# Rows in runs of 16 m tiles, 36 longer transfers, and an earlier start of the engines, in a matmul-and-subtract kernel

**Chip, cores, metric.** One core of a Trainium2 chip. The time is device microseconds of one execution; every kernel was run several times beside the kernel before on the same chip. "Span" is the length of one execution in the record; each run's time is 1.7 to 1.9 us above its own span (2.0 to 2.1 in e10_order8).

## The reference

```python
batch, m, k, n = 16, 512, 1024, 768
x = randn(batch, m, k); weight = randn(k, n); sub_value = randn(batch, m, n)   # all float32
out = np.matmul(x, weight) - sub_value
```

Flattened, x is 8192 x 1024: 64 m tiles of 128 rows. The kernel reads 61.9 MB and writes 25.2 MB whatever its order, so the bytes of its loads and stores cannot be reduced.

## The kernel before

SyncE issues every transfer, in the order of one list: x tiles, weight chunks (`w`), sub tiles (`s`) and stores (`o`). ScalarE casts an x tile to fp16; TensorE transposes it (VectorE does so for two tiles in six); TensorE multiplies it with the resident weights; VectorE subtracts out of PSUM into the sub tile's own buffer, from which it is stored.

```python
S = 8                      # rows of a run: partition p holds the rows of S m tiles, one after the other
TRANSFERS = [              # (kind, first tile, tiles)
    ('x', 0, 1), ('w', 0, 1), ('x', 1, 1), ('w', 1, 1), ('x', 2, 1), ('w', 2, 1),
    ('x', 3, 2), ('w', 3, 1), ('s', 0, 1), ('x', 5, 3), ('s', 1, 3), ('x', 8, 4),
    # ... 38 in all, at most 8 tiles each ...
    ('o', 61, 2), ('o', 63, 1),
]
# ...
x_s = x_flat.rearrange("(s p j) k -> s p j k", p=P, j=S)     # the same for sub_value and out
section.enter_context(tc.tile_critical(no_gpsimd_drain=True))  # SyncE opens the section
# ...
# the operands of the idle matmuls, which keep TensorE busy until data is there: cleared by VectorE
dve.add(lambda: nc.vector.memset(idle_w, 0.0), then=count("idle"))
dve.add(lambda: nc.vector.memset(idle_x, 0.0), then=count("idle"))
# ...
idle(13)                  # 13 matmuls on zeros, a fourteenth follows below
cast(0)
# ...
# each of PE, DVE, ACT visits the block "past" at the end of its program once before its work:
with nc.body("turn_head", valid_engines=engines):
    nc.br_cmp(turn, 0, on_true="past", on_false="work", comp_op="IS_EQ", engines=engines)
with nc.body("work", valid_engines=engines):
    for q in (act, dve):
        q.emit(q.ops)
    # ... TensorE's program, most of it a loop over six tiles ...
with nc.body("past", valid_engines=engines):
    nc.regs_alu(turn, turn, 1, op=mybir.AluOpType.add)
    nc.br_cmp(turn, 2, on_true="turn_head", on_false="rest", comp_op="IS_LT", engines=engines)
```

Of the kernel before, what the change touches and what calls it, by code (L numbers as in the profile page):

```python
# [10 lines left out]
F32 = mybir.dt.float32  # L11
F16 = mybir.dt.float16

S = 8
NX, NSO = 16, 32
N16, NXT, NPT, NPO = 4, 4, 2, 3
N16P, NXTP = 2, 1
# [5 lines left out]
PER = 6  # L23
HEAD = 3
ON_DVE = frozenset(range(10, 60, 6))
HEAD_SLOT = None
LOOP = (4, 6, 10)

TRANSFERS = [
    ('x', 0, 1), ('w', 0, 1), ('x', 1, 1), ('w', 1, 1), ('x', 2, 1), ('w', 2, 1),  # L30
    ('x', 3, 2), ('w', 3, 1), ('s', 0, 1), ('x', 5, 3), ('s', 1, 3), ('x', 8, 4),
    ('s', 4, 4), ('x', 12, 4), ('s', 8, 8), ('x', 16, 2), ('x', 18, 6), ('s', 16, 8),
    ('x', 24, 8), ('o', 0, 8), ('s', 24, 8), ('x', 32, 8), ('s', 32, 8), ('x', 40, 8),
    ('o', 8, 8), ('o', 16, 8), ('s', 40, 8), ('x', 48, 8), ('s', 48, 8), ('x', 56, 8),
    ('o', 24, 8), ('o', 32, 8), ('s', 56, 8), ('o', 40, 8), ('o', 48, 8), ('o', 56, 5),
    ('o', 61, 2), ('o', 63, 1),
]


class Queue:  # L40
# [28 lines left out]
    def emit_loop(self, bodies):  # L69
# [30 lines left out]

        with self.nc.Fori(0, len(bodies), engines=OrderedEngineSet([self.engine.engine]), head_slot=HEAD_SLOT):
            self.emit(first, value=lambda sem, v: regs[sem.name], after=after)
# [3 lines left out]
def kernel(  # L106
# [7 lines left out]
    nc = tc.nc  # L114
# [11 lines left out]

    x_s = x_flat.rearrange("(s p j) k -> s p j k", p=P, j=S)
    sub_s = sub_flat.rearrange("(s p j) n -> s p j n", p=P, j=S)
    out_s = out_flat.rearrange("(s p j) n -> s p j n", p=P, j=S)
    w_c = weight.rearrange("(c p r) n -> c p r n", p=P, r=2)  # L130

    section = ctx.enter_context(ExitStack())
    section.enter_context(tc.tile_critical(no_gpsimd_drain=True))  # L133

    def sbuf(name, shape, dtype):
        return ctx.enter_context(nc.sbuf_tensor(name, shape, dtype)).ap()
# [13 lines left out]
    idle_w = sbuf("idle_w", [P, P], F16)  # L150
    stub = sbuf("stub", [P, 2], F16)
    mark = sbuf("mark", [P, 1], F32)
    idle_x = sbuf("idle_x", [P, 512], F16)
# [8 lines left out]
    def count(name):  # L162
        so_far[name] += 1
        return (counter[name], 1)

    sp, pe = Queue(nc, nc.sync), Queue(nc, nc.tensor)
    act, dve, pool = Queue(nc, nc.scalar), Queue(nc, nc.vector), Queue(nc, nc.gpsimd)

    pool.add(lambda: nc.gpsimd.memset(ident, 0.0), then=count("ident"))  # L169
    pool.add(lambda: nc.gpsimd.affine_select(  # L170
        out=ident, in_=ident, compare_op=mybir.AluOpType.not_equal, fill=1.0, base=0,
# [52 lines left out]
    def issue():  # L224
        nonlocal known
        while todo:
# [30 lines left out]
            here = ring[:, at % size : at % size + n]  # L257
            there = view[at // S][:, at % S : at % S + n]
            waits = []
# [23 lines left out]
    def cast(mi):  # L283
# [4 lines left out]
        waits = [landed["x", mi]]  # L288
        if first in ON_DVE:
            if mi == first:  # L290
# [14 lines left out]
    def transposes(mi):  # L305
        def one(c):
            def f():
                waits = []
                if c == 0:
                    b, before = take("pt", NPT, mi)  # L310
                    waits.append((counter["cast"], cast_at[mi]))
                    if before is not None:
                        waits.append((counter["evac"], evac_at[before]))
                b = slot["pt", mi]
                words = pt_b[:, b].bitcast(F32)[:, c * P : (c + 1) * P]
                from_ = x16_b[:, slot["x16", mi]].bitcast(F32)[:, c * P : (c + 1) * P]
                last = c == n_c - 1
                pe.add(lambda: nc.tensor.transpose(words, from_, ident), waits, count("turn") if last else None)  # L318
                if last:
                    turn_at[mi] = so_far["turn"]  # L320
                    waits = [(counter["turn"], turn_at[mi])]
                    if mi - mi % 2 == EARLY:
                        if mi == EARLY:
                            take("xtp", NXTP, mi)
                        to = xtp_b[:, slot["xtp", EARLY], mi - EARLY]
                    else:
                        d, before = take("xt", NXT, mi)
                        if before is not None:
                            waits.append((counter["mul"], mul_at[before]))
                        to = xt_b[:, d]  # L330
                    act.add(lambda: nc.scalar.copy(out=to, in_=pt_b[:, b]), waits, count("evac"))  # L331
                    evac_at[mi] = so_far["evac"]
            return f
        return [one(c) for c in range(n_c)]

    def transposes_dve(mi):

        x16 = x16p_b[:, slot["x16p", mi]].bitcast(F32).rearrange("p j (c q) -> p (j c) q", c=n_c)
        blocks = [(a, b) for a in range(P // Q) for b in range(P // Q)]

        def one(n, a, b):
            def f():
                waits = []
                if n == 0:
                    d, before = take("xtp", NXTP, mi)
                    waits.append((counter["cast"], cast_at[mi + 1]))
                    if before is not None:
                        waits.append((counter["mul"], mul_at[before + 1]))
                xt = xtp_b[:, slot["xtp", mi]].bitcast(F32).rearrange("p j (c m) -> p (j c) m", c=n_c)
                last = n == len(blocks) - 1  # L350
                dve.add(lambda: nc.vector.transpose(  # L351
                    xt[b * Q : (b + 1) * Q, :, a * Q : (a + 1) * Q],
                    x16[a * Q : (a + 1) * Q, :, b * Q : (b + 1) * Q],
                ), waits, count("pair") if last else None)
                if last:
                    pair_at[mi] = so_far["pair"]
            return f
        return [one(n, a, b) for n, (a, b) in enumerate(blocks)]

    def matmuls(mi, c):  # L360
        first = mi - mi % 2
        on_dve = first in ON_DVE or first == EARLY
        waits = []
# [31 lines left out]
    def finish(mi):  # L395
        assert mi in done["s"]
        done["finish"].add(mi)
        o = so_ring[:, mi % NSO].rearrange("p (h n) -> p h n", h=2)
        po = po_b[:, slot["po", mi]]
        dve.add(lambda: nc.vector.tensor_tensor(  # L400
            out=o, in0=po[:, :, :NS], in1=o, op=mybir.AluOpType.subtract
        ), [landed["s", mi], (counter["mul"], mul_at[mi])], count("finish"))
        finish_at[mi] = so_far["finish"]
        issue()
# [1 line left out]
    issue()  # L406


    starts = len(dve.ops)
    dve.add(lambda: nc.vector.memset(idle_w, 0.0), then=count("idle"))  # L410
    dve.add(lambda: nc.vector.memset(idle_x, 0.0), then=count("idle"))  # L411
    dve.ops = dve.ops[starts:] + dve.ops[:starts]

    def idle(n):
        pe.add(lambda: nc.tensor.ldweights(idle_w, tile_position=(0, 0)), [(counter["idle"], 2)])  # L415
        for _ in range(n):
            pe.add(lambda: loaded_matmul(po_b[:, NPO - 1, 0], idle_w, idle_x, start=True, stop=True))

    def lead(mi):
        return LEAD_DVE if mi - mi % 2 in ON_DVE else TA + CA  # L420

# [51 lines left out]
    for mi in range(HEAD + (EARLY is not None), n_mt):  # L473
# [3 lines left out]
        t = mi + TA  # L477
        tr = transposes(t) if ahead <= t < n_mt and t - t % 2 not in ON_DVE else []
        for c in range(n_c):
# [9 lines left out]
        finish(mi)  # L489
        if mi + LEAD_TURN in ON_DVE:  # L490
            waiting += transposes_dve(mi + LEAD_TURN)
# [14 lines left out]
    with nc.body("turn_head", valid_engines=engines):  # L506
        nc.br_cmp(turn, 0, on_true="past", on_false="work", comp_op="IS_EQ", engines=engines)  # L507
    with nc.body("work", valid_engines=engines):
        for q in (act, dve):
            q.emit(q.ops)  # L510
        first, size, times = LOOP
        pe.emit(pe.ops[: marks[first]])
        ends = [marks[first + size * n] for n in range(times + 1)]
        pe.emit_loop([pe.ops[a:b] for a, b in zip(ends, ends[1:])])
        pe.emit(pe.ops[ends[-1] :])
        nc.br("past", engines=engines)
    with nc.body("past", valid_engines=engines):
        nc.regs_alu(turn, turn, 1, op=mybir.AluOpType.add)  # L518
        nc.br_cmp(turn, 2, on_true="turn_head", on_false="rest", comp_op="IS_LT", engines=engines)  # L519
    nc.switch_bb("rest")  # L520

    left = [one for one in lanes if not one["tags"] <= known]
    last = next(one for one in left if of_o[n_mt - 1] in one["tags"])
# [36 lines left out]
```

## Time and profile before

| | before |
|---|---|
| time, median of the six runs beside the kernel after | 210.94 us (210.65 to 211.54) |
| span of the profiled run | 208.7 us |
| TensorE busy, DMA queue busy | 94%, 97.9% |
| idle matmuls begin | 6.07 us |
| last matmul ends | 204.05 us |
| last subtraction ends, last store lands | 205.04 us, 207.4 us |

In the profiled run the last store, of one tile, needs 2.3 us from its issue to its landing, and from the landing to the end are 1.3 us. The profiled run took 210.46 us. The prediction shows the page's lines.

### The profile page before, as it was taken

The numbers are of one execution on the slowest core, as the hardware profiler recorded it, in microseconds if no ns is written. First come the engines' busy times: TensorE is split into PE (matmuls) and PEld (weight loads), VectorE is DVE, ScalarE is ACT, GpSimd is POOL, SyncE is SP. The second block draws the span as 40 slices with busy tenths as digits, with TensorE's granted clock in tenths as the row PEclk, the third lists the DMA queues.
The fourth block names the chain that finished last, engine by engine and source line by source line (L and its number), as shares of the span: only waits on it lengthen the run. The fifth ranks groups of instructions, "written<-read, shape, count | busy, mean of one in ns | idle before, by whom it ended". The sixth has DMA issues, their size and how long they took to land.

```text
span 208.7 us, 2630 instructions
## 1 busy us (share of the span) xinstructions
PE 196.2 (94%) x1234; PEld 75.6 (36%) x700; DVE 127.6 (61%) x218; ACT 108.9 (52%) x113; POOL 0.8 (0%) x7
## 2 busy tenths in 40 slices
PE   0899979999999999999999999999999999999991
PEld 0023324434433443443443344344344334434430
DVE  0231151995696599299469559929946955982331
ACT  2246478554762845557276284555727629434510
POOL 1000000000000000000000000000000000000000
PEclk9999999999999999999999999999999999999997
DMA  6999999999999999999999999999999999999985
GB/s 205 407 426 429 436 422 433 443 419 437 438 422 457 400 438 443 446 427 407 460 433 415 424 429 433 441 440 432 416 452 415 435 424 429 438 438 419 423 350 211
DMA packets 5476, 87.08 MB, mean 417 GB/s; under 512 B 608, under 2 KB 608, under 8 KB 1888
## 3 DMA queue, kind: packets, MB, share of 16 engines
q1 hardware_dynamic: 5472, 87.03, 97.9%
q14 instruction: 3, 0.02, 0.1%
q8 instruction: 1, 0.02, 0.0%
HBM read 61.87 MB, written 25.17 MB: 417 GB/s over the span
## 4 chain that ended last, share of the span: by engine, by line
PE 92%; ACT 3%; issue 2%; DVE 1%; DVEq 0%; SPq 0%
PE po_b L181 82%; PE pt_b L318 10%; ACT x_b L300 1%; ACT xt_b L331 1%; ACT xtp_b L331 0%; DVE so_ring L400 0%; DVE idle_x L411 0%; DVE idle_w L410 0%; DVEq L507 0%; DVEq L519 0%; DVEq L518 0%; DVEq L555 0%; DVEq L504 0%; SPq L133 0%
## 5 line engine op out<-in xcount | busy, mean ns | idle before, releaser
L181 PE MATMUL po_b<-w_sb,xt_b 128*128 128x384 f16 x704 | 125.9, 326 | 0.0
L400 DVE TENSOR_TENSOR so_ring<-po_b,so_ring 128x768 f32<-128x768 f32 x64 | 61.2, 958 | 60.0 <-PE po_b L181 53.8
L331 ACT COPY xt_b<-pt_b 128x1024 f16<-128x1024 f16 x44 | 44.5, 1012 | 80.3 <-PE pt_b L318 79.0
L351 DVE STREAM_TRANSPOSE xtp_b<-x16p_b 32x256 f32<-32x256 f32 x144 | 62.7, 435 | 2.2
L181 PE MATMUL po_b<-w_sb,xtp_b 128*128 128x384 f16 x320 | 61.3, 326 | 0.1
L380 PEld LDWEIGHTS <-xt_b 128*128 128x128 f16 x352 | 34.4, 98 | 57.2 <-issue 53.7
L318 PE MATMUL pt_b<-ident,x_b 128*128 128x128 f32 x184 | 47.6, 274 | 1.6 <-ACT x_b L300 1.4
L300 ACT CAST x_b<-x_ring 128x1024 f16<-128x1024 f32 x46 | 47.2, 1048 | 2.9 <-DMA x_ring<-in_x_dram 2.9
L318 PEld LDWEIGHTS pt_b<-ident,x_b 128*128 128x128 f32 x184 | 25.4, 141 | 46.1 <-issue 42.4
L380 PEld LDWEIGHTS <-xtp_b 128*128 128x128 f16 x160 | 15.7, 98 | 18.5 <-issue 16.4
L300 ACT CAST x16p_b<-x_ring 128x1024 f16<-128x1024 f32 x18 | 18.8, 1046 | 4.0 <-DMA x_ring<-in_x_dram 4.0
L181 PE MATMUL po_b<-idle_x,idle_w 128*128 128x512 f16 x26 | 9.2, 513 | 6.1 <-DVE idle_x L411 6.1
L248 DVE CAST w_sb<-so_ring 128x768 f16<-128x768 f32 x8 | 4.1, 556 | 9.6 <-DMA so_ring<-in_weight_dram 9.6
L410 DVE MEMSET idle_w<- 128x64 uint32 x1 | 0.1, 112 | 5.6 <-issue 5.6
L331 ACT COPY xtp_b<-pt_b 128x1024 f16<-128x1024 f16 x2 | 2.0, 1012 | 2.2 <-PE pt_b L318 2.2
L415 PEld LDWEIGHTS <-idle_w 128*128 128x128 f16 x4 | 0.4, 99 | 6.1 <-DVE idle_x L411 6.1
L300 ACT ACT_TABLE_LOAD x1 | 1.3, 1283 | 1.8 <-issue 1.8
L487 ACT CAST stub<-ident 128x1 f16<-128x1 f32 x2 | 0.4, 196 | 0.0
L170 POOL TENSOR_SCALAR_AFFINE_SELECT ident<-ident 128x128 f32<-128x128 f32 x1 | 0.3, 292 | 0.1
L411 DVE MEMSET idle_x<- 128x256 uint32 x1 | 0.3, 272 | 0.0
L464 POOL MEMSET mark<- 128x1 f32 x1 | 0.1, 99 | 28.6 <-ACT xtp_b L331 28.6
L169 POOL MEMSET ident<- 128x128 f32 x1 | 0.2, 204 | 0.5 <-SPq L133 0.5
(4 smaller groups left out, 0.4 us busy)
## 6 DMA issues: line engine op xcount, KB each, us to landing
so_ring<-in_sub_value_dram SPq DMA_DIRECT2D x7, 3072.0 KB, 24.3
out_dram<-so_ring SPq DMA_DIRECT2D x7, 3072.0 KB, 24.5
x_ring<-in_x_dram SPq DMA_DIRECT2D x5, 4096.0 KB, 20.7
x_ring<-in_x_dram SPq DMA_DIRECT2D x2, 2048.0 KB, 27.1
so_ring<-in_weight_dram SPq DMA_DIRECT2D x4, 768.0 KB, 9.6
x_ring<-in_x_dram SPq DMA_DIRECT2D x1, 3072.0 KB, 24.8
x_ring<-in_x_dram SPq DMA_DIRECT2D x2, 1024.0 KB, 23.2
out_dram<-so_ring SPq DMA_DIRECT2D x1, 1920.0 KB, 7.7
```

Source lines behind the costliest of these rows:

```text
L170: pool.add(lambda: nc.gpsimd.affine_select(out=ident, in_=ident, compare_op=mybir.AluOpType.not_equal, fill=1.0, base=0, pattern=[[-1, P]] ...
L181: return nc.tensor.add_instruction(mybir.InstMatmult(name=nc.get_next_instruction_name(), engine=full.engine, ins=list(full.ins), outs=lis ...
L248: lambda at=at, r=r, st=st: nc.vector.tensor_copy(out=w_sb[:, at, r], in_=st[:, r]),
L300: act.add(lambda: nc.scalar.copy(out=to, in_=x_in), waits, count("cast"))
L318: pe.add(lambda: nc.tensor.transpose(words, from_, ident), waits, count("turn") if last else None)
L331: act.add(lambda: nc.scalar.copy(out=to, in_=pt_b[:, b]), waits, count("evac"))
L351: dve.add(lambda: nc.vector.transpose(xt[b * Q : (b + 1) * Q, :, a * Q : (a + 1) * Q], x16[a * Q : (a + 1) * Q, :, b * Q : (b + 1) * Q],), ...
L380: pe.add(lambda weights=weights: nc.tensor.ldweights(weights, tile_position=(0, 0)), [w for w in waits if w[0] in ready])
L400: dve.add(lambda: nc.vector.tensor_tensor(out=o, in0=po[:, :, :NS], in1=o, op=mybir.AluOpType.subtract), [landed["s", mi], (counter["mul"] ...
L411: dve.add(lambda: nc.vector.memset(idle_x, 0.0), then=count("idle"))
L415: pe.add(lambda: nc.tensor.ldweights(idle_w, tile_position=(0, 0)), [(counter["idle"], 2)])
L487: lambda t=t: nc.scalar.copy(out=stub[:, t - n_mt : t - n_mt + 1], in_=ident[:, :1]), [(counter["ident"], 2)], count("cast")
```

## The change

Its intent: TensorE should start earlier (GpSimd clears the idle operands, VectorE's visit comes nearer, GpSimd lets the engines into the section), and the memory traffic should need fewer and longer transfers.

```diff
-S = 8
+S = 16
+NEAR = 140
 TRANSFERS = [
     ('x', 0, 1), ('w', 0, 1), ('x', 1, 1), ('w', 1, 1), ('x', 2, 1), ('w', 2, 1),
-    ('x', 3, 2), ('w', 3, 1), ('s', 0, 1), ('x', 5, 3), ('s', 1, 3), ('x', 8, 4),
-    ... 38 in all
+    ('w', 3, 1), ('x', 3, 2), ('s', 0, 4), ('x', 5, 2), ('x', 7, 5), ('s', 4, 4),
+    ('x', 12, 4), ('s', 8, 8), ('x', 16, 2), ('x', 18, 8), ('s', 16, 4), ('s', 20, 12),
+    ('x', 26, 6), ('o', 0, 16), ('x', 32, 5), ('s', 32, 6), ('x', 37, 6), ('x', 43, 5),
+    ('s', 38, 10), ('o', 16, 10), ('x', 48, 8), ('s', 48, 10), ('x', 56, 8), ('o', 26, 6),
+    ('o', 32, 16), ('s', 58, 6), ('o', 48, 10), ('o', 58, 4), ('o', 62, 1), ('o', 63, 1),
 ]
-    section.enter_context(tc.tile_critical(no_gpsimd_drain=True))
+    section.enter_context(tc.tile_critical(sync_engine=mybir.EngineType.Pool, no_gpsimd_drain=True))
+    pool.add(lambda: nc.gpsimd.memset(idle_w, 0.0), then=count("idle"))
+    pool.add(lambda: nc.gpsimd.memset(idle_x, 0.0), then=count("idle"))
-    dve.add(lambda: nc.vector.memset(idle_w, 0.0), then=count("idle"))     # (cut: moved to VectorE's front)
-    dve.add(lambda: nc.vector.memset(idle_x, 0.0), then=count("idle"))
-        for q in (act, dve):
-            q.emit(q.ops)
+        act.emit(act.ops)
+        dve.emit(dve.ops[:NEAR])
     nc.switch_bb("rest")
+    dve.emit(dve.ops[NEAR:])
```

## The prediction

> **What bounds the kernel now.** I read the busy shares first, then the stages, then the head of the chain of work that ended last, then single instructions of the head.
>
> The page's busy shares, its slices for the DMA, and its queue table:
>
> ```profile
> PE 196.2 (94%) x1234; PEld 75.6 (36%) x700; DVE 127.6 (61%) x218; ACT 108.9 (52%) x113; POOL 0.8 (0%) x7
> ...
> DMA  6999999999999999999999999999999999999985
> ...
> q1 hardware_dynamic: 5472, 87.03, 97.9%
> ```
>
> Two resources are full at once. TensorE is busy 94% of the span, and the DMA queue 97.9% of it. The stage table tells whether the DMA share is an average or holds everywhere (columns: stage, length, busy time of PE, PEld, DVE, ACT, POOL, granted clock, DMA share, GB/s):
>
> ```profile
> 0.00:20.00 20.00, 13.78 (x60) 2.98 (x28) 4.50 (x10) 7.65 (x8) 0.70 (x6) 1.00 0.92 365
> 20.00:40.00 20.00, 18.36 (x119) 7.39 (x70) 8.05 (x12) 13.40 (x15) 0.10 (x1) 1.00 1.02 431
> 40.00:80.00 40.00, 40.00 (x260) 15.93 (x147) 30.35 (x55) 22.82 (x24) 0.00 (x0) 1.00 1.01 431
> ...
> 120.00:160.00 40.00, 40.00 (x261) 16.23 (x150) 28.18 (x49) 24.17 (x25) 0.00 (x0) 1.00 1.01 433
> 160.00:200.00 40.00, 40.00 (x261) 16.12 (x149) 26.15 (x44) 19.88 (x23) 0.00 (x0) 1.00 1.00 429
> 200.00:209.00 9.00, 4.04 (x25) 1.08 (x11) 1.92 (x2) 0.00 (x0) 0.00 (x0) 0.86 0.58 239
> ```
>
> From 40 to 200 us TensorE is never idle, and from 20 to 200 us the DMA never is: it moves 429 to 433 GB/s in every stage, 431 on average. So neither bound has room in the middle. What can move lies in the first 30 us and in the last 6. The head of the chain:
>
> ```profile
> 1.04 0.06 DVEq L507
> 1.11 3.99 issue
> 5.10 0.05 DVEq L518
> ...
> 5.63 0.11 DVE idle_w L410
> 5.74 0.28 DVE idle_x L411
> 6.03 0.05 issue
> 6.07 6.09 PE po_b L181 x14
> 12.17 0.45 PE pt_b L318 x4
> ```
>
> VectorE jumps to the block at the end of its program (L507) and comes out of the jump 3.99 us later (L518). Only then does it clear the operands of the idle matmuls, so TensorE's fourteen idle matmuls begin at 6.07 us and hold it until 12.17, although the first x tile was cast by 6.95 us (cast from 5.91, 1.04 long). The first real transposes are therefore some 4 to 5 us late.
>
> **What the Trainium skill says.** "Runtime: NRT & Kernel Launch", section Instruction fetch mechanics: a taken branch to a target outside the resident window of two 16 KiB pages has to fetch the target before it goes on. The trace agrees with a stall of this kind: VectorE's jump costs 3.99 us, while ScalarE, whose program is shorter, is at the same block (1.0 to 1.4 us) within 0.4 us. "TensorE: Matmul & The Clock Gate", Part 1: a cold array runs at half rate and warms after about 3.4 us of activity counted in a free-running window. The trace agrees with the half rate, 6.09 us / 14 = 435 ns for an idle matmul of 512 columns at first and 1.24 us / 5 = 248 ns in the next group; it shows about 6 us to the change here. "DMA: Bandwidth & Descriptors", section Where 436 GB/s comes from: the SBUF side has a ceiling of 435 GB/s. The trace's 431 stands at 99% of that.
>
> **The change part by part.**
>
> *GpSimd clears the idle operands.* Two clears of 0.11 and 0.27 us leave VectorE, and GpSimd gets them ahead of its identity. GpSimd begins that identity at 0.94 us and clears 128x128 f32 in 0.20 us, so I estimate both clears done by 1.5 us. TensorE is through its own two branches at about 2.25 us (the second starts at 1.9, the longer takes 0.34). So the idle matmuls start at about 2.3 in place of 6.07: 3.75 us earlier. They end at about 8.4, after the cast at 6.95 and after w chunk 0 is cast at 8.82 or nearly.
>
> *VectorE visits mid-program.* Its first 140 operations come before the visited block and the rest after it, so the target is about as near as ScalarE's, whose visit is cheap. I expect the 4 us to vanish. Even if they stayed, nothing needs VectorE before w chunk 0 lands at 7.79.
>
> *GpSimd enters the section for all engines.* The five engines start at 0.8 to 0.9 us now; the gate moves from SyncE to GpSimd. I expect 0 to 0.1 us at the start, and at most 0.2 at the end, partly beside the last store.
>
> *The transfers.* The bytes are the same, 87.03 MB; there are 36 transfers in place of 38 (estimate, from the sizes of both lists). A line fits the arrivals in before: arrival = 5.5 us + MB queued up to and including it / 0.431. It gives 23.4 for x tiles 5 to 7 (7.73 MB; measured 6.70 + 16.7 = 23.4), 34.7 for sub tiles 4 to 7 (12.58 MB; measured 8.22 + 26.5 = 34.7) and 98.0 for x tiles 32 to 39 (39.85 MB; measured 73.42 + 24.6 = 98.0). For the new order:
> - w chunk 1 at 11.2, x tile 2 at about 12.4 and w chunk 2 at 14.3 are unmoved. With TensorE 3.75 us earlier, matmuls of chunk 1 (16.01 before) would start at 12.26; that chunk is cast by 12.23. Those of chunk 2 (19.04 before) would start at 15.29; it is cast at 15.38. So up to here 3.65 of the 3.75 us are kept.
> - w chunk 3 moves ahead of x tiles 3 and 4, which now land where the chunk did, at 18.7. Cast of tile 3 ends at 19.75, so its transposes start at 19.8 against 22.29: 2.5 us are kept.
> - Then the chain of before repeats: transposes, copy 1.01, cast 0.95, transposes of tile 4 at 22.4, copy to 24.1. x tiles 5 and 6 come at 5.5 + 8.39/0.431 = 25.0 (24.1 would have been wanted), cast to 25.95, transposes of tile 5 at 26.0 against 27.65: 1.65 us are kept.
>
> From there TensorE works without a gap, as now, so its last matmul ends at 204.05 - 1.65 = 202.4. I checked the later arrivals against this earlier clock with the same line. x tiles 32 to 36 come at 5.5 + 41.42/0.431 = 101.6, where ScalarE wants to cast tile 34 at 96.1. It stands for 5.5 us, but the copy behind it (tile 30) ends near 103.5, and matmuls of tile 30 start at about 105. So nothing reaches TensorE, with 1.5 us to spare.
>
> *The sum.* TensorE's side: 208.7 - 1.65 = 207.05 us of span. The DMA's side: at 200 us before had moved 7.31 + 8.62 + 17.24 + 17.29 + 17.33 + 17.15 = 84.94 MB (the stage rates, taken to two digits). The 2.09 MB left need 4.85 us at 431 GB/s, to 204.85. The last store takes 2.3 us from issue to landing, of which 0.9 is moving 0.39 MB, so 1.4 us follow: 206.25. From the last landing (205.1 + 2.3 = 207.4) to the end before has 1.3 us: 207.55. The later of the two sides rules, 207.55 at most; fewer short runs at the head (one sub transfer of four tiles for one of a single tile) may give some 0.2 back, so I take 207.2 to 207.5. The timed median lies 211.03 - 208.7 = 2.33 us above the span, which makes 209.5 to 209.8. I say 209.5.
>
> **The rivals.**
>
> *The whole head gain survives.* The 3.75 us at the start reach the end: about 207.3. For it speaks only that the idle matmuls are the first wait of the chain. Against it speak the arrivals above, and that the DMA would need 87.03 MB in 2 us less, at 435 GB/s or more, when no stage of before passes 433.
>
> *Nothing survives.* The DMA is the only bound, or TensorE's gain goes into waits for x: 211. For it: 97.9% of the queue busy. Against it: the last stage shows 239 GB/s, so the stores at the end wait for TensorE, and the DMA has about 2 us of slack there.
>
> *Runs of 16 rows change the rate of the memory.* Each partition's rows lie twice as far apart when a transfer has fewer than 16 m tiles. 1% of rate is 2 us, either way: 207.5 or 211.6. No view of before can tell.
>
> *The VectorE stall moves to mid-program.* If crossing into the last part costs the 4 us later, its transposes (they end at 46.6, wanted at 48.57: 2 us of slack) would make TensorE stand 2 us once: about 211.
>
> **Range and chances.** The main estimate 209.5 holds if the rate of before holds. Half a per cent of rate is 1 us; the head may be off by 1 us, as arrivals there are known to about 0.3 us and follow in a chain of casts. I put 8 in 10 on 207.5 to 211.2. Two per cent faster is below 206.81, which needs both the whole head gain and a rate above the ceiling of before: 0.05. Two per cent slower is above 215.25, which needs a stall that nothing shows: 0.02. Within: 0.93.
>
> **What would show it right or wrong.** Right: the idle matmuls begin near 2.3 us; no issue gap of 4 us at VectorE's visit; TensorE waits at tiles 3 and 5 for casts that wait for x; tile 5's transposes begin near 26.0; TensorE's last matmul ends near 202.4; the stages between 20 and 200 us stay at 429 to 435 GB/s; the final stage has a higher rate than 239. Wrong: a middle stage off 431 by over 1% (then the row runs matter), waits of TensorE after 40 us (a late x or sub transfer, or the stall moved), idle matmuls still near 6 us (TensorE's own branches or GpSimd are late), or an end that comes more than 1.5 us after the last landing (the GpSimd exit costs).

## The result and the profile after

| | before | after | predicted for after |
|---|---|---|---|
| time, median of six | 210.94 us | 211.12 us (210.83 to 211.30) | 209.5 us |
| idle matmuls begin | 6.07 | 2.06 | 2.3 |
| w chunk 0 has landed | 7.8 | 8.9 | 7.8 |
| last matmul ends | 204.05 | 203.27 | 202.4 |
| last subtraction ends | 205.04 | 204.26 | 203.4 |
| last store lands | 207.4 | 208.1 | 206.25 |
| span | 208.7 | 209.5 | 207.2 to 207.5 |

The ratio of after to before is 1.0005 (95% interval 0.999 to 1.002): the same. Ratios here are the mean time of one kernel's fast runs over that of the other's fast runs of the same rounds, so they are not quite the ratio of the medians quoted. The time forecast, 1.5 us less, was wrong, although 211.12 still lies inside the range.

TensorE did start 4 us earlier. The timeline of the head, kernel after (start, duration, engine, line, operation, and in brackets the idle time before it and what ended it):

```profile
0.97 0.20 POOL L169 MEMSET idle_w<- 128x128 f16 x1 [0.53 <-POOLq L133]
1.11 0.53 POOL L170 MEMSET idle_x<- 128x512 f16 x1
...
2.06 5.73 PE L183 MATMUL po_b<-idle_x,idle_w 128*128 128x512 f16 x14 [2.06 <-POOL idle_x L170]
...
8.94 1.03 DVE L250 CAST w_sb<-so_ring 128x768 f16<-128x768 f32 x2 [8.94 <-DMA so_ring<-in_weight_dram]
...
25.77 1.04 ACT L302 CAST x_b<-x_ring 128x1024 f16<-128x1024 f32 x1 [0.66 <-DMA x_ring<-in_x_dram]
```

The clears are done and the idle matmuls run by 2.06 us. VectorE is out of its jump at 1.6 us (5.1 before). But the first weight chunk is there at 8.94 us; the same line of before reads 7.79. The cast of x tile 5, which had been expected to start at 25.0 us, starts at 25.77.

The waits of TensorE, kernel after (engine, line, waited for, us in total, times, longest):

```profile
PE pt_b L320 <- ACT x_b L302: 3.1, 3, 1.7
PE po_b L183 <- POOL idle_x L170: 2.1, 1, 2.1
PE po_b L183 <- DVE w_sb L250: 1.1, 2, 0.7
PE po_b L183 <- DVE so_ring L402: 0.3, 1, 0.3
```

The one wait of 6.1 us for the idle operands has become 2.1 us. Other waits have taken back 3.1 of these 4 us: those for casts of late x tiles are 3.1 us (1.4 before), for weights 1.1 (none before), for a subtraction 0.3 (none before). From 40 us on there is no wait, as before. So TensorE keeps 204.05 - 203.27 = 0.78 us of its 4.

The stage table, kernel after, in the form that the prediction explains:

```profile
0.00:20.00 20.00, 16.14 (x74) 3.47 (x34) 4.11 (x8) 7.85 (x8) 1.30 (x8) 1.00 0.92 356
20.00:40.00 20.00, 17.06 (x109) 7.06 (x68) 7.92 (x12) 14.27 (x15) 0.10 (x1) 1.00 1.02 433
40.00:80.00 40.00, 40.00 (x259) 15.86 (x147) 31.10 (x56) 22.25 (x24) 0.00 (x0) 1.00 1.02 435
...
160.00:200.00 40.00, 40.00 (x260) 15.96 (x148) 25.21 (x42) 19.86 (x22) 0.00 (x0) 1.00 1.00 430
200.00:210.00 10.00, 3.26 (x21) 0.88 (x9) 1.92 (x2) 0.00 (x0) 0.00 (x0) 0.93 0.56 233
```

The rate from 20 to 200 us is that of before. The first stage moves 356 GB/s against 365, which is 0.18 MB or 0.4 us of transfer less. And the last stage, with 2.33 MB left (2.15 before), has no higher rate than before (233 over 10 us, 239 over 9).

Now the end. The last store, from the view of the DMA, before and then after (size, us from issue to landing):

```profile
out_dram<-so_ring SPq DMA_DIRECT2D x1, 384.0 KB, 2.3
```

```profile
out_dram<-so_ring SPq DMA_DIRECT2D x1, 384.0 KB, 3.9
```

After the change the last tile's store is handed over 0.8 us earlier and lands 0.8 us later: it stands 1.6 us behind other stores. The page's averages do not tell how this queue looks from inside. The trace does: it records sixteen increments of a semaphore for each transfer, one for each of the sixteen DMA engines. The table gives these sixteen landings for some transfers (worked out from the trace; MB is what the list has moved up to and including the transfer, two numbers where before and after differ):

| transfer | MB | before: first, middle, last | after: first, middle, last |
|---|---|---|---|
| w chunk 0 | 1.31 | 5.89, 6.25, 7.77 | 6.07, 6.37, 8.91 |
| x tiles 16, 17 | 18.87 | 47.31, 47.64, 49.43 | 47.69, 47.98, 50.26 |
| x tiles 56 to 63 | 68.16 / 69.73 | 161.43, 161.79, 163.53 | 165.44, 165.80, 168.09 |
| last store | 87.03 | 207.19, 207.28, 207.37 | 206.41, 206.51, 208.14 |

For most of the run fourteen of the sixteen landings are within 1 us of each other, while the last comes some 2 us (before) or 2.6 us (after) behind the first: at w chunk 0 it is 1.88 us in before and 2.84 in after. Towards the end a third one falls behind too. These increments do not name their engine; the packet records do, as shown under e8 below. A transfer counts as landed when the last engine has brought its share. In before the last store has its sixteen landings within 0.2 us, since the queue was empty when it came. In after, earlier stores are still under way on the late engine; the first engine is done at 206.4, the last one 1.7 us later. This is where the gain went.

### The profile page after: what moved, and what is told of

It is laid out like the page before. It is cut to its first block, busy times and chain, and to the rows that moved or that the text cites. A ratio compares the mean times of both kernels' runs of the same rounds, so it can differ in the third digit from the quotient of the medians.

```text
span 209.5 us, 2628 instructions
## 1 busy us (share of the span) xinstructions
PE 196.5 (94%) x1234; PEld 75.4 (36%) x700; DVE 126.9 (61%) x216; ACT 109.1 (52%) x113; POOL 1.4 (1%) x9
## 3 DMA queue, kind: packets, MB, share of 16 engines
q1 hardware_dynamic: 5184, 87.03, 97.7%
## 4 chain that ended last, share of the span: by engine, by line
PE 84%; DMA 9%; SPq 3%; ACT 1%; DVE 0%; issue 0%; POOLq 0%
PE po_b L183 75%; DMA x_ring<-in_x_dram 9%; PE pt_b L320 9%; SPq L283 2%; SPq L247 1%; ACT x_b L302 1%; DVE so_ring L402 0%; SPq L553 0%; POOLq L133 0%; POOLq L542 0%
## 5 line engine op out<-in xcount | busy, mean ns | idle before, releaser
L170 POOL MEMSET idle_x<- 128x512 f16 x1 | 0.5, 528 | 0.0
```

Of the source, the lines that this page charges most:

```text
L170: pool.add(lambda: nc.gpsimd.memset(idle_x, 0.0), then=count("idle"))
```

## The experiments

The theory that the experiments test (A): the end is set by the slowest DMA engine's stream of equal shares, and instruction fetches amid the first loads decide how late that engine starts. Rivals: the new rows and transfers eat the gain (B); the exit through GpSimd, or something after the stores, costs it (C).

All runs in one table. "w0" is the landing of w chunk 0; "sub" the end of the last subtraction, "store" the landing of the last store, both in the profiled run.

| run | w0 | sub | store | store - sub | median us | ratio to before (95%) |
|---|---|---|---|---|---|---|
| before | 7.77 | 205.04 | 207.37 | 2.33 | 210.94 | |
| after | 8.91 | 204.26 | 208.14 | 3.88 | 211.12 | 1.0005 (0.999 to 1.002) |
| e1_engines | 7.74 | 202.99 | 207.51 | 4.52 | 210.73 | 0.9993 (0.9982 to 1.0005) |
| e2_transfers | 8.82 | 204.68 | 208.19 | 3.51 | 211.20 | 1.0011 (0.9996 to 1.0025) |
| e3_visit_end | 8.76 | 204.10 | 208.09 | 3.99 | 211.20 | 1.0019 (1.0005 to 1.0034) |
| e4_clears | 8.45 | 203.75 | 207.67 | 3.92 | 210.78 | 0.9997 (0.9985 to 1.0009) |
| e7_rows | 8.68 | 204.83 | 208.46 | 3.63 | 211.60 | 1.0027 (1.0012 to 1.0043) |
| e10_order8 | 8.08 | 204.86 | 208.27 | 3.41 | 211.79 | 1.0039 (1.0006 to 1.0072) |
| e8_no_visit | 6.56 | 202.81 | 207.53 | 4.72 | 210.73 | 0.9987 (0.9954 to 1.002) |
| e12_after_no_visit | 6.81 | 204.42 | 208.53 | 4.11 | 211.42 | 1.0019 (1.0006 to 1.0031) |
| e11_late_start | 8.26 | 203.54 | 208.13 | 4.59 | 212.18 | 1.0064 (1.0048 to 1.0079) |
| e5_before_half | 7.71 | 203.70 | 206.03 | 2.33 | 209.22 | 0.9919 (0.990 to 0.9938) |
| e6_after_half | 8.99 | 204.34 | 206.67 | 2.33 | 209.73 | 0.9936 (0.9915 to 0.9957) |
| e9_engines_half | 7.63 | 202.82 | 205.16 | 2.34 | 209.18 | 0.9913 (0.9901 to 0.9926) |

The column "store - sub" is the test of what bounds the end. Where the queue is empty it is 2.33 us; everything above is waiting behind the late engine. "sub" moves over 2 us among the kernels with all their bytes, and "store" does not follow it. The last two stores show that the late engine has no gap there: in every kernel with all its bytes except before, the last landing of the last store comes 0.92 to 0.96 us after the last landing of the store ahead of it, and 0.39 MB at 431 GB/s take 0.9. In before it is 1.12 us: the late engine stood still for some 0.2 us (an estimate from these numbers), so in that run no more than this was to be won at the end without a shorter stream.

### The parts of the change, one at a time

**e1_engines**: the engine parts alone.

```diff
-S = 16            # and the 36 transfers
+S = 8             # and the 38 transfers of before; the rest as after
```

> The change's engine parts alone (GpSimd clears and gate, VectorE visits mid-program), with the rows and transfers of before. Theory A, the DMA stream sets the end: its slowest engine starts late because instruction fetches of the new visit come amid the first loads. Then w chunk 0 arrives near 8.9 us as after the change (7.8 before), TensorE's last matmul ends near 202 to 203, the last store lands near 208 and the time is 211.0 to 211.4, although the transfers are those of before. Theory B, the new rows and transfers eat the gain: then w chunk 0 arrives near 7.8, the span is about 207.2 and the time 209.3 to 209.8.

Measured: 210.73 us, ratio 0.9993. w chunk 0 came at 7.74 us (8.9 expected), so this part of theory A was wrong: the engine parts alone do not delay it. TensorE won 2.05 us, more than in the full change. Its last subtraction, and the last store's way:

```profile
202.03 0.96 DVE L403 TENSOR_TENSOR so_ring<-po_b,so_ring 128x768 f32<-128x768 f32 x1 [1.64 <-PE po_b L184]
```

```profile
out_dram<-so_ring SPq DMA_DIRECT2D x1, 384.0 KB, 4.5
```

All results are there at 202.99 us, 2.05 us before the kernel before has them, yet the last store lands at 207.51, 0.14 us later than before. Theory B predicted 209.8 or less for this run, and it has none of B's rows and transfers. B is out as the main cause: with the old transfers the gain is lost as well.

**e4_clears**: GpSimd's clears alone, all else as before.

```diff
-    dve.add(lambda: nc.vector.memset(idle_w, 0.0), ...)     # and idle_x
+    pool.add(lambda: nc.gpsimd.memset(idle_w, 0.0), ...)    # and idle_x; kernel before otherwise
```

> The kernel before with one part alone: GpSimd clears the idle operands; the visit at the end, the gate on SyncE, rows and transfers as before. Theory A: idle matmuls start near 2.1 us and TensorE ends 1.5 us or more before 204.05, yet the last store lands near 207.1 to 207.4 because the stream is full to its end; time 210.5 to 211.0, so under 0.3% faster. Theory B (the head gain is real and only the new transfers lost it): last store 2 us or more earlier, time 209.3 or less.

Measured: 210.78 us, ratio 0.9997; TensorE's end 1.3 us earlier (1.5 or more had been expected), the last store at 207.67, 0.3 us later than in before. The same picture: an earlier TensorE, and a store that does not come earlier.

**e2_transfers**: rows and transfers alone, engines of before. **e7_rows**: the rows alone.

```diff
-S = 8
+S = 16            # e2: also the 36 transfers; e7: the 38 transfers of before
```

> The change's rows and transfers alone, with the engines of before. Theory A: w chunk 0 arrives near 7.8 us as before, idle matmuls start near 6.1, the last store lands near 207.4 and the time is 210.7 to 211.1. Theory B: w chunk 0 arrives near 8.9 us and the time is 211.6 or more, as TensorE starts as late as before and the stream is slower too.

> The kernel before with runs of 16 rows alone, its own transfers kept. Theory A1, the row runs delay the first loads: w chunk 0 arrives near 8.8 us in place of 7.8, later arrivals are 0.5 to 1 us late, the last store lands near 208 and the time is 211.2 to 211.6. Theory A2, only the new order of transfers or chance of the instruction fetches delays them: w chunk 0 arrives between 7.7 and 8.5, the time is 210.7 to 211.0.

Measured: e2 at 211.20 us (1.0011), e7 at 211.60 us (1.0027). In both, w chunk 0 comes near 8.75 us, and the last store lands 0.8 and 1.1 us later than in before. The expectation of A for e2 missed; of B its late chunk came, and its time of 211.6 or more did not. A1 for e7 held. So the runs of 16 rows do cost something, at the head. The change is the sum of a part that wins nothing (engines, 0.9993) and rows that lose 0.3%; e2 against e7 suggests that the new list wins some 0.15% back, but the two ran on different chips and the intervals overlap, so that is not settled.

**e3_visit_end**: the kernel after, with VectorE's visit at the end of its program.

```diff
-NEAR = 140
+NEAR = 1000
```

> The kernel after, but VectorE visits the end of its program as before (all its operations before the visited block). Theory A: fetches fall as before, VectorE stands about 4 us in its jump but nothing needs it before 7.8 us; w chunk 0 arrives near 7.8, arrivals are about 0.5 to 0.9 us earlier than after the change, the last store lands near 207.2 to 207.5 and the time is 210.2 to 210.7. Theory B: w chunk 0 stays near 8.9 and the time at 211.1, within 0.2.

Measured: 211.20 us, w chunk 0 at 8.76. The expectation of A missed, and B's numbers came: the place of VectorE's visit makes no difference to the loads here. So for the end of the kernel theory A stands (e1, e4), while for the late head the 16-row runs are involved (e2, e3, e7 all have them, and w chunk 0 near 8.75). Whether through the fetches or by themselves is what e8 and e12 below tell apart.

### Is it the bytes?

**e5_before_half**, **e6_after_half**, **e9_engines_half**: three kernels (before, after, e1_engines) with half of the late sub columns not loaded. Their outputs are wrong, which doesn't matter for the times.

```diff
             there = view[at // S][:, at % S : at % S + n]
+            if kind == "s" and at >= 32:
+                here, there = here[:, :, : N // 2], there[:, :, : N // 2]
```

> The kernel before with the sub loads of tiles 32 to 63 cut to half their columns (6.3 MB or 14.6 us of transfer less; wrong result on purpose). Theory A, before is bound by TensorE and the DMA stream nearly together: TensorE's end stays at 204.0, the last store lands 2.0 to 2.3 us after the last subtraction, the span is 208.3 to 208.7 and the time 210.4 to 210.8: at most 0.2% faster. If the stream alone were the bound the time would fall by 2 us or more.

> The kernel after with the same cut (wrong result on purpose). Theory A, after is bound by the DMA stream at its end: TensorE's end stays near 203.3, but the last store now lands 2.0 to 2.3 us after the last subtraction in place of 3.9, so the span falls from 209.5 to 207.5 to 207.9 and the time to 209.6 to 210.1, 0.3 to 0.5% below the other half kernel. Theory C (the exit through GpSimd or something after the stores costs): time stays at 211.1.

> The change's engine parts with the transfers and rows of before, with the same cut (wrong result on purpose). Theory A: TensorE ends near 202.0, nothing holds the last store, the span is 206.3 to 206.7 and the time 208.4 to 208.9, about 1% below the kernel before: this is the head gain that the full stream of bytes hides. Theory C: 210.7 as without the cut.

Measured: 209.22, 209.73 and 209.18 us. In all three the wait behind other stores is gone (2.33 us, column "store - sub"). e6 came as expected, except that it was to be 0.3 to 0.5% faster than e5 and was 0.2% slower. It settles C: the exit is the same, and the time falls by 1.4 us. (With the gate on GpSimd the end comes 1.37 us after the last landing, with SyncE 1.30, in all runs to 0.01: the exit costs 0.07 us.)

The other two missed, each in a useful way. e5 fell by 1.9 us and not by 0.2, because TensorE's end came at 202.7 and not at 204.0. The head gives the likely reason. The first line is that of e5, the second that of the profiled run of before:

```profile
5.84 4.86 PE L181 MATMUL po_b<-idle_x,idle_w 128*128 128x512 f16 x14 [5.84 <-DVE idle_x L413]
```

```profile
6.07 6.09 PE L181 MATMUL po_b<-idle_x,idle_w 128*128 128x512 f16 x14 [6.07 <-DVE idle_x L411]
```

The same fourteen matmuls took 4.86 us here and 6.09 there (4.57 to 6.09 over all runs). They are slow until TensorE's clock rises (its warm-up), which came at 9.25 us in e5 and at 11.97 in before. TensorE's waits are otherwise nearly the same in both (5.8 and 1.4 us in e5, 6.1 and 1.4 in before). So the profiled run of before probably had a late warm-up, and in runs with an early one the DMA stream would hide TensorE's earlier end; that is inferred from this one pair of profiles. By the same pair, 1.3 of the 2.05 us that TensorE won in e1 against the profiled run of before may be no more than that. e9 was expected at 208.4 to 208.9 and came to 209.18, no faster than e5. Only its profiled run (208.34) showed the gain of the engine parts: 206.5 us of span against 207.3. So even without the DMA bound the head gain is 0.8 us in one pair of profiles and nothing in the medians; which of the two is typical stays open.

### Is it the instruction fetches?

**e8_no_visit**: e4_clears without any visit of a later block. **e12_after_no_visit**: the same edit in the kernel after.

```diff
-    nc.regs_mov(turn, 0)
+    nc.regs_mov(turn, 1)
```

> GpSimd's clears, rows and transfers of before, and no engine visits a later block at all. If instruction fetches amid the loads make one or two DMA engines lag, the fetches now come later and apart: the lag of the last of the sixteen engines at w chunk 0 falls below 1.3 us (1.5 in before, 1.9 with the clears alone) and rises by 0.4 to 1 us at each later fetch; the end depends on their number: 210.3 to 210.9. VectorE or ScalarE may stand some us at a fetch in mid-program, hidden or not. If fetches have nothing to do with the lag, it stays at 1.5 to 1.9 us at w chunk 0.

> The kernel after with no visit of a later block on any engine; rows and transfers as after. If its late first loads (w chunk 0 at 8.9 us) come from instruction fetches amid them, w chunk 0 arrives near 6.6 as without the visit on runs of 8 rows (6.56), and the lag of the last of the sixteen engines there falls from 2.5 us to 0.4; TensorE ends near 202; the fetches come later and the last store still lands at 207.4 to 208.1, time 210.6 to 211.1. If the runs of 16 rows themselves slow the first loads, w chunk 0 arrives at 7.3 or later with the sixteen engines close together.

The queues between 1 and 12 us, from the view of the DMA: kernel after first, then e8_no_visit (packets, MB, share of the sixteen engines):

```profile
q1 hardware_dynamic: 803, 3.67, 91.0%
q14 instruction: 2, 0.02, 0.6%
q8 instruction: 1, 0.02, 0.5%
```

```profile
q1 hardware_dynamic: 867, 4.01, 92.7%
```

Three instruction fetches (two of 8 KiB, one of 16 KiB) fall between the first loads of the kernel after; without the visit there is none, and 0.34 MB more data has been moved (0.17 MB more than in before, which has the list of e8). The head gains what the fetches had cost it, as both expectations said for that case: w chunk 0 is there at 6.56 us in e8 and 6.81 in e12, against 8.45 and 8.91 with the visits. Here the sixteen engines are within 0.64 and 0.79 us of each other.

The fetches are not gone, though; they come later. This is the same view of e8 between 29 and 35 us:

```profile
q1 hardware_dynamic: 203, 2.59, 102.1%
q8 instruction: 1, 0.02, 1.1%
```

One fetch of 16 KiB, at 30.9 us. The last of the sixteen landings was 0.42 us behind the middle in the transfer that landed at 29.6 us, and 1.41 us behind in the one at 34.3: a step of 1.0 us, and it stays.

The packet records tell which engine pays. In this stretch each packet starts within 0.02 us of the end of another one. Linked in this way they form sixteen chains, one for each DMA engine, and each chain carries eight packets of every transfer and one of 4 bytes. A fetch stands in one of the chains, in the place of data. In e8 the chain with the 16 KiB fetch goes from 0.07 us ahead of the middle one to 1.46 us behind it, a delay of 1.5 us; the 8 KiB fetches at 57.0, 79.5 and 160.9 us delay theirs by 0.9, 0.6 and 1.0. In the kernel after, the 16 KiB fetch of 5.18 us stands in the chain that is the latest from w chunk 0 to the end (2.2 to 2.4 us behind the middle), and the 8 KiB fetches of 4.64 and 162.8 us both stand in the second latest (1.1 us behind, then 2.1); the one of 3.32 us, amid the first transfer, leaves no lasting delay (0.1).

Fetches are not the whole lag. One chain without a fetch falls behind by up to 0.6 us with most of the stores: in e8 from the middle at 71 us to 1.9 us behind it at the end, in after to 1.8. In e8 two chains also lose 0.4 and 0.6 us between 176 and 183 us, where the trace shows no fetch. Why is not shown. By the end three chains of e8 are 1.9 to 2.2 us behind the middle (the last landing in before: 1.7), and the last store lands at 207.53.

So the fetches cause most of the last engine's lag (1.5 of its 2.2 us in e8), and where they come decides when it is paid. e8 has the earliest loads of all and an end at 210.73 us, the same as before. e12 is at 211.42: its last store, 208.53, is 0.4 us beyond what had been expected. TensorE ended at 203.42 and not near 202; its clock stood at 0.57 of full in the stretch from 25 to 29 us (as in e10 from 26 to 30), but the last store waits for the late engine all the same. That engine is 1.0 us behind that of e8 at the end. Half of it, 0.5 us, is there when x tile 1 lands (8.34 against 7.83), while the two lists are still the same. The gate differs as well, but over the other runs it is the rows that tell: the first of the sixteen landings of x tile 1 comes at 7.18 to 7.42 us with runs of 8 rows, whatever the gate (without e11, which starts late), and at 7.49 to 7.64 with runs of 16. So this is the cost of the 16-row runs on the first loads. Why rows twice as far apart slow them is not shown. The rest comes mostly with the fetches: the one of 16 KiB moves the last landing by 1.3 us here and by 1.0 in e8.

Rows and fetches together cost more than each alone. Without the visits w chunk 0 comes 0.25 us later with 16 rows (e12 against e8); with them it comes at 7.63 to 8.45 us in the kernels with 8 rows and at 8.68 to 8.99 in those with 16. Why they add up in this way is not shown either.

**e11_late_start**: e4_clears, with the first load held back until the clears are done, so that fetches come ahead of the data.

```diff
+            if (kind, at) == ("x", 0):
+                waits.append((counter["idle"], 2))
             sp.add(lambda here=here, there=there: nc.sync.dma_start(out=here, in_=there), waits, (sem, 16))
```

> The clears alone (e4_clears) with the first load held until GpSimd's two clears are done, near 1.65 us in place of 0.9, so that the first instruction fetches (at 2.0 us) come before the data. The stream starts 0.7 to 0.8 us later; if the fetches then cost the engines nothing, the final lag falls from 2.3 to about 1.5 us and the last store lands within 0.3 us of 207.6, time 210.5 to 210.9. If the fetches cost as much as before, the last store lands near 208.4, time 211.4 to 211.6.

Measured: a miss. In the profiled run (211.23 us) the last landing at the end was 1.5 us behind the middle one and 2.0 behind the first (1.9 and 2.3 in e4), and the last store came at 208.13, between the two forecasts: what is won is less than the later start costs. The other runs were slower, up to 212.81 us with a median of 212.18, above both forecasts, and no trace shows why.

### Shorter runs with the new order

**e10_order8**: the kernel after with runs of 8 rows, and its transfers cut where such a run ends: 46 of them.

```diff
-S = 16
+S = 8
-    ('x', 7, 5), ... ('s', 20, 12), ... ('o', 0, 16), ...
+    ('x', 7, 1), ('x', 8, 4), ... ('s', 20, 4), ('s', 24, 8), ... ('o', 0, 8), ('o', 8, 8), ...
```

> The kernel after with runs of 8 rows again: its engine parts and its order of transfers, each transfer cut where a run of 8 ends (46 transfers). If the runs of 16 rows delay the first loads, w chunk 0 arrives near 7.7 us (8.9 after), all arrivals follow 0.5 to 1 us earlier, the last store lands near 207.4 and the time is 210.4 to 210.8. If the longer transfers and not the rows were what costs or gains, it stays at 211.1 or goes up.

Measured: 211.79 us, ratio 1.0039: a miss for the rows, while the other case named, that the time goes up, came. w chunk 0 was earlier than in after (8.08, 7.7 expected), but the last store came at 208.27. Transfers have a price of their own. If the landing of each transfer on the fastest engine is taken and the bytes so far at 434.5 GB/s are subtracted, the rest grows by 0.06 to 0.07 us with nearly every load, after one of 0.39 MB as after one of 4.2 MB, and unevenly around the stores (e8: from 2.84 us for the first to 4.81 for the thirty-eighth). Each transfer is eight packets and one of 4 bytes on each engine, whatever its size, so this may be a cost of packets. Eight transfers more than in e1 are an estimated 0.5 us, of the 0.76 us by which the store is later. Another 0.2 us of e10 lie outside the span (2.0 us between span and time in place of 1.8); where they come from is not shown.

No version beat both kernels by more than the intervals. Those at 210.73 are e1_engines and e8_no_visit.

## Why the prediction was wrong

- **The head of TensorE: right.** The stall of VectorE does not hold TensorE any more, and the idle matmuls began at 2.06 us (2.3 said).
- **The arrivals: right in kind, off in size.** The chain of waits at tiles 3 and 5 is the one described. But the line for arrivals was carried over from before, with the lateness of the last engine there. After the change the late engine was 1.1 us later at w chunk 0 and 0.8 to 0.9 us later from there on: w chunk 1 at 12.08 in place of 11.2, x tiles 5 and 6 at 25.75 in place of 25.0. The 1.65 us were 0.78.
- **"The DMA's side" of the sum: this step failed.** It counted what all sixteen engines together had moved by 200 us, and let the rest run at their common rate to 204.85. The end waits for the last engine, which is 2 us behind that mean. The text had the right tool in hand: its own line for arrivals counts landings on the last engine, and at 87.03 MB it gives 5.5 + 87.03/0.431 = 207.4, exactly the landing measured in before (207.37). With the head 0.9 us later that makes 208.3; measured 208.14. So the DMA's side was 1.9 us too early: 1.15 of it from counting the mean in place of the last engine, the rest from the later head. Applied to the end, the line would have said that nothing can be gained.
- **From span to time, 2.33 us:** this took the median of some runs less the span of another. Apart from e10 each run is some 1.8 us above its own span, and the profiled run of before was 0.5 us faster than the median. It decides nothing here.
- **The rival "Nothing survives" was what happened.** It was turned down because 239 GB/s in the last stage looked like 2 us of slack. It was slack of the fast engines only: their landings before the last store were 2 us ahead.
- **"The whole head gain survives":** out, by e1: 2.05 us kept by TensorE to its end (some of it perhaps the warm-up, see e5), none by the time.
- **"Runs of 16 rows change the rate":** not the rate (429 to 435 GB/s in all stages), but the first loads, 0.5 us, and e7 shows 0.3% of time.
- **"The VectorE stall moves to mid-program":** not seen. A fetch does come at 162.8 us, and one more DMA engine is later from there on (1.1 us behind the middle at 158.4 us, 2.1 at 168.1), but TensorE does not wait.
- **Later x tiles:** x tiles 32 to 36 came at 102.5 (101.6 said), and nothing reached TensorE, as said.
- **The exit: right.** From the last landing to the end 1.30 us before and 1.37 after (at most 0.2 more said).

## What to carry to other kernels

When a kernel's DMA queue is full from the first byte to the last, starting the compute earlier may buy nothing, as here; ask when the last share of the last store can land, not when the mean rate says that the bytes are through. A mean over sixteen engines can hide one that is never idle: compare the landing of the last store with that of a store into an empty queue (here 2.33 us after its subtraction), since whatever it takes longer is queue. And before blaming the new part of a change, run its other part alone: here both lost the gain in the same place.

## What the Trainium skill lacked or had wrong

- "Runtime: NRT & Kernel Launch", Instruction fetch mechanics: it calls the cost of crossing a page boundary mostly hidden. It was hidden from TensorE (no wait after 40 us), but not from a full DMA stream: a 16 KiB fetch put one DMA engine 1.5 us behind for good, 8 KiB fetches 0.6 to 1.0 us (e8). The page has nothing on fetches delaying the data that share their DMA engine (w chunk 0 at 6.56 us without them, 8.45 with).
- "DMA: Bandwidth & Descriptors", Why a DMA increments its semaphore by 16 and not by 1: that the engines finish independently agrees with the trace. How far apart they can stay is not said: some 2 us (before) to 2.6 us (after) from the first to the last, from the head to the last stores.
- "DMA: Bandwidth & Descriptors", Where 436 GB/s comes from: the ceiling of 435 agrees with the 434.5 GB/s between landings. That for transfers between HBM and the SBUF the HBM's side (about 358) binds does not hold here, with one core running: 429 to 435 GB/s in the stages from 20 to 200 us of the kernel after. The page lacks that each transfer in a full queue costs some 0.06 us besides, whatever its size.
- "TensorE: Matmul & The Clock Gate", Part 1: that the warm-up varies from run to run agrees (4.57 to 6.09 us for the same fourteen matmuls), but it varies by more than the 500 ns either way that the page gives: from the first idle matmul to the rise of the clock it took 2.8 us in e1_engines and 5.9 us in before.
- No page says how much later loads come when a partition's rows are twice as far apart in memory: 0.5 us on the last landing of the third load here (e12 against e8), with no cause shown.
